# A gated encoder layer on one core: gate and up projections with the activation stationary instead of the weights

## The chip, the cores and the metric

The kernel runs on one core of a Trainium2 chip. The metric is the device time of one execution in microseconds. The time before is the median of three runs.

## The reference

One layer over 256 tokens of width 2048: a gated feed-forward network (FFN), two token mixers side by side with a gated merge, and a second FFN, each with norms around it. The change touches the two FFNs only.

```
def swiglu(h, w_gate, w_up, w_down):
    return (jax.nn.silu(h @ w_gate) * (h @ w_up)) @ w_down
...
f = swiglu(rmsnorm(x, ffn1_pre_g[l]), ffn1_w_gate[l], ffn1_w_up[l], ffn1_w_down[l])
x = x + 0.5 * rmsnorm(f, ffn1_post_g[l])
...
f = swiglu(rmsnorm(x, ffn2_pre_g[l]), ffn2_w_gate[l], ffn2_w_up[l], ffn2_w_down[l])
x = x + 0.5 * rmsnorm(f, ffn2_post_g[l])
```

w_gate and w_up are 2048 x 5632, w_down is 5632 x 2048, all float32.

## The kernel before

Every float32 operand is split into a high part (fp32r) and a low part, the rest. A product is three matmuls: high by high, low by high, high by low, summed in PSUM. The weights stream from memory once, in 728 **units** of 512 KB, in the order in which blocks use them (`add_block`, `add_block_T`). SyncE issues the loads (L147). ScalarE makes the high part of a unit (`whi`, L159) and VectorE the low part (`wlo`, L161). There are four buffers for the loaded unit (`raw`) and ten for the split ones, so five units are in store.

The 256 tokens are two halves `h` of 128. `xT` holds the transposed, split activations, 16 tiles of 128 rows by 256 tokens, in high and low. The norm's factor per token, `r_pre`, is not in `xT`; it is applied to the products.

There are two ways to run a block.

- `run_block` (L195): the activation is **stationary** (128 x 128) and 512 weight columns **move**. A unit is 256 rows by 512 columns. Per unit there are two halves, two row tiles and three matmuls (`mm3`, L169 to L171): 12 matmuls of 512 columns. A block over 2048 rows has 8 units, so 96 matmuls. The result has tokens on partitions and FFN columns along the free axis. All of the mixers, the down projections and the first 512 FFN columns (c == 0) run so.
- `run_block_T` (L225): the weights are **stationary**. A unit is 512 rows by 256 columns. The moving operand is `xT`: 512 columns (high and low of 256 tokens) against `whi`, then 256 columns (the high part) against `wlo`. A block makes 256 FFN columns for all tokens in 32 such pairs (L238 and L239; the last of each PSUM tile the other way round, L241 and L242). The result has FFN columns on partitions, which is the form in which the down projection wants its stationary operand, so nothing is transposed. The columns c = 1 to 10 of each FFN (512 wide, so two blocks `q` each for gate and for up) run so.

For c == 0, `up_after` multiplies (VectorE, L400) and `split_T` transposes the product on TensorE (L310), four tiles for each half, copies and splits it (L312, L313). For the other columns `sum_T` adds the two halves of a PSUM tile, a broadcast `r_bc` of the norm's factor is multiplied in (L415, L421), and silu, product and split follow. `r_bc` is made once for each FFN by `make_r_bc`, with two transposes (L372).

The FFN runs in two halves of its columns: gate and up of c = 0 to 5, their down projection, gate and up of c = 6 to 10, their down projection. The order on each engine is a schedule that is worked out when the kernel is built; the engines then run their queues in order.

Of the kernel before, what the change touches and what calls it, by code (L numbers as in the profile page):

```python
# [17 lines left out]
P = 128  # L18
# [24 lines left out]
def encoder_layer(  # L43
# [30 lines left out]
    def acc_tile():  # L74
        return accp.tile([P, NC], F32, tag="acc", name=nm("acc"))
# [26 lines left out]
    ident_r = const.tile([P, P], F32R, name="ident_r")  # L102
    sink = const.tile([P, NQ], F32, name="sink")
    nsink = const.tile([P, NQ], F32, name="nsink")
    r_bc = const.tile([P, SEQ], F32, name="r_bc")
    nlam = const.tile([P, 1], F32, name="nlam")
    mhalf = const.tile([P, 1], F32, name="mhalf")

# [12 lines left out]
    def add_block(w, r0, nu, c0):  # L121
        start = len(units)
        for u in range(nu):
            units.append(w[r0 + 256 * u:r0 + 256 * u + 256, c0:c0 + NC])
        return start

    def add_block_T(w, c0):
        start = len(units)
        for u in range(4):
            units.append(w[NC * u:NC * (u + 1), c0:c0 + 256])  # L130
        return start

    loaded, emitted = {}, {}
# [30 lines left out]
    def weights(k):  # L164
        emit_upto(k + LA)
        return emitted[k]
# [12 lines left out]
    def pump():  # L179
        for d in list(deferred):  # L180
            d[0] -= 1
            if d[0] <= 0:
                deferred.remove(d)
                d[1]()
        if ticker[0] is not None:
            try:
                next(ticker[0])
            except StopIteration:
                ticker[0] = None
# [31 lines left out]

    def quad(t, u):
        return t[:, :, 2 * (u % 2):2 * (u % 2) + 2, :]

    def run_block_T(start, after):  # L225
        """acc[m] = [W_m^T x_hi | W_m^T_hi x_lo] for two column tiles m of 128, tokens along the free axis."""
        acc = [acc_tile(), acc_tile()]
        for i in range(4):
            whi, wlo = weights(start + i)
            whi, wlo = (w.rearrange("p a b -> p (a b)").rearrange("p (j c) -> p j c", c=256) for w in (whi, wlo))  # L230
            for j in range(4):
                k = 4 * i + j
                xt = xT[k // 2][:, :, k % 2, :]
                for m in range(2):
                    a = whi[:, j, m * P:(m + 1) * P]
                    b = wlo[:, j, m * P:(m + 1) * P]
                    if k < 15:
                        nc.tensor.matmul(acc[m], a, xt, start=k == 0, stop=False)  # L238
                        nc.tensor.matmul(acc[m][:, 0:SEQ], b, xt[:, 0, :], start=False, stop=False)  # L239
                    else:  # L240
                        nc.tensor.matmul(acc[m][:, 0:SEQ], b, xt[:, 0, :], start=False, stop=False)  # L241
                        nc.tensor.matmul(acc[m], a, xt, start=False, stop=True)  # L242
            pump()
        after(acc)

    def rsqrt_of(ss, mul, add, tag):
        w = ss.shape[-1]
# [111 lines left out]
                nc.vector.tensor_tensor(fv, src, gb, ALU.mult)  # L359
            post_norm(f, pw, h, final)  # L360

    def sum_T(t, acc):
        for m in range(2):
            nc.scalar.copy(t[:, m], acc[m][:, SEQ:NC])  # L364
            nc.vector.tensor_tensor(t[:, m], acc[m][:, 0:SEQ], t[:, m], ALU.add)  # L365

    def make_r_bc():
        tp = tp_tile()
        for h in range(2):
            b = t2()[:, 0:P]  # L370
            nc.vector.tensor_copy(b, r_pre[h].to_broadcast([P, P]))
            nc.tensor.transpose(tp[:, h, :], b, ident)  # L372
        nc.vector.tensor_copy(r_bc.rearrange("p (h t) -> p h t", t=P), tp[:, 0:2, :])

    def ffn(post_g, pre, plan, lag, final, tail):
        hT = {}

        def hT_of(gu, h):
            if gu < 2:
                return quad(hT[0, h], gu)  # L380
            return hT[gu][:, :, :, h * P:(h + 1) * P]

        f = [[g4([2 * NC], F32) for _ in range(2)] for _ in range(2)]
        ss = [small(4, f"fss{h}") for h in range(2)]

        def lhs_h(off):
            return lambda u, h: hT_of(off + u, h)

        for half, (c_lo, c_hi) in enumerate(((0, 6), (6, 11))):
            for c in range(c_lo, c_hi):  # L390
                if c == 0:
                    s = [None, None]

                    def gate_after(h, acc):
                        s[h] = t2()
                        nc.scalar.activation(s[h], acc, AF.Silu, scale=r_pre[h])

                    def up_after(h, acc):
                        hh = t2()
                        nc.vector.scalar_tensor_tensor(hh, acc, r_pre[h], s[h], ALU.mult, ALU.mult)  # L400

                        def tr(h=h, hh=hh):
                            hT[0, h] = split_T(hh, 4, [2, 4, P])
                        later(tr, 1)
                    run_block(plan["gate"][c], KU, lhs_x, gate_after, lag, pre)
                    run_block(plan["up"][c], KU, lhs_x, up_after)
                    make_r_bc()
                    continue
                for q in (2 * c, 2 * c + 1):
                    st = [None]  # L410

                    def gate_T(acc):
                        t = st[0] = t2().rearrange("p (m t) -> p m t", t=SEQ)
                        sum_T(t, acc)
                        nc.vector.tensor_tensor(t, t, r_bc.unsqueeze(1).to_broadcast([P, 2, SEQ]), ALU.mult)  # L415
                        nc.scalar.activation(t, t, AF.Silu)

                    def up_T(acc):
                        t = t2().rearrange("p (m t) -> p m t", t=SEQ)
                        sum_T(t, acc)  # L420
                        nc.vector.tensor_tensor(t, t, r_bc.unsqueeze(1).to_broadcast([P, 2, SEQ]), ALU.mult)  # L421
                        nc.vector.tensor_tensor(t, t, st[0], ALU.mult)
                        o = hT[q] = g4([2, 2, SEQ])
                        nc.scalar.copy(o[:, 0], t)
                        nc.vector.tensor_tensor(o[:, 1], t, f32(o[:, 0]), ALU.subtract)
                    run_block_T(plan["gT", q], gate_T)
                    run_block_T(plan["uT", q], up_T)
            nu = 2 * (c_hi - c_lo)
            for n in range(4):
                gb = load_bc(post_g[0, n * NC:(n + 1) * NC]) if half == 1 else None  # L430
                last = half == 1 and n == 3

                def down_after(h, acc, n=n, gb=gb, last=last, half=half):
                    if half == 0:
                        nc.scalar.copy(f[h][n // 2][:, (n % 2) * NC:(n % 2) * NC + NC], acc)
                        return
                    finish_f(acc, f, gb, ss[h], h, n, True, 4.0 / D, 4.0 * EPS, final)
                run_block(plan["down"][half][n], nu, lhs_h(2 * c_lo), down_after, (LAG_END if final else LAG) if last else 0,
                          tail=tail if last else None)

    def plan_ffn(w_gate, w_up, w_down):
        pl = {"gate": {}, "up": {}, "down": [[], []]}
        for half, (c_lo, c_hi) in enumerate(((0, 6), (6, 11))):
            for c in range(c_lo, c_hi):
                if c == 0:
                    pl["gate"][c] = add_block(w_gate[0], 0, KU, 0)
                    pl["up"][c] = add_block(w_up[0], 0, KU, 0)
                    continue
                for q in (2 * c, 2 * c + 1):
                    pl["gT", q] = add_block_T(w_gate[0], q * 256)  # L450
                    pl["uT", q] = add_block_T(w_up[0], q * 256)
            for n in range(4):
                pl["down"][half].append(add_block(w_down[0], c_lo * NC, 2 * (c_hi - c_lo), n * NC))
        return pl
# [343 lines left out]


def _constants():  # L800
    """Rotary tables [cos, cos, -sin, sin] and window masks: functions of the shapes alone."""
    inv = np.float32(10000.0) ** (-np.arange(0, HD, 2, dtype=np.float32) / np.float32(HD))
    ang = np.arange(SEQ, dtype=np.float32)[:, None] * inv[None, :].astype(np.float32)
    c, s = np.cos(ang).astype(np.float32), np.sin(ang).astype(np.float32)
    rope = np.concatenate([c, c, -s, s], axis=1).reshape(2, P, 256).transpose(1, 0, 2)
    i = np.arange(P)
    keep = np.stack([i[None, :] <= i[:, None], i[None, :] >= i[:, None]], axis=1)
    mask = np.where(keep, np.float32(0), np.float32(NEG)).astype(np.float32)
    return np.ascontiguousarray(rope), np.ascontiguousarray(mask)
# [19 lines left out]
```

## Time and profile before

| | |
|---|---|
| runs | 2098.62, 2098.82, 2098.98 us, median 2098.82 us |
| profiled execution, span from first to last instruction | 2097.0 us |
| TensorE matmul busy | 2080.2 us, 99% |
| TensorE weight load busy | 1757.2 us, 84% |
| VectorE busy | 1253.5 us, 60% |
| ScalarE busy | 990.1 us, 47% |
| memory read | 187 GB/s over the span |

The profile gives the profiled execution's time as its span alone; it is 1.8 us under the median of the runs. Busy time of TensorE counts overlapped matmuls once, but the durations of single matmuls overlap their neighbours. What a matmul takes on the path is therefore read from start to start.

### The profile page before, as it was taken

What the parts mean: (1) busy time and instruction counts of PE and PEld (TensorE: products, weight loads), DVE (VectorE), ACT (ScalarE), POOL (GpSimd) and SP (SyncE); (2) the same over time, 40 slices, a digit from 0 to 9 for tenths busy, and PEclk for the clock granted to TensorE, in tenths of its full rate; (3) what the DMA queues carried; (4) which work ended last, traced back from release to release, by engine and by line L of the source; (5) the groups of instructions that cost most, each with busy time, mean ns of one, the idle gap of its engine ahead of it and who ended that gap; (6) DMA issues with size and microseconds to landing.
All of it is one profiled execution on the core that took longest, in us unless ns stands there. A gap on an engine that the chain in (4) does not pass through costs nothing.

```text
span 2097.0 us, 27165 instructions
## 1 busy us (share of the span) xinstructions
PE 2080.2 (99%) x10497; PEld 1757.2 (84%) x10497; DVE 1253.5 (60%) x1576; ACT 990.1 (47%) x1365; POOL 24.5 (1%) x41
## 2 busy tenths in 40 slices
PE   9999999999999999999999999999999999999998
PEld 6888888888888878888888888788888888888886
DVE  5665654456565576767755555666666445666655
ACT  6544444444444455554644444554444444444442
POOL 1000000000000000000000000000000000000000
PEclk9999999999999999999999999999999999999999
DMA  7665666666566656555466666566665666665663
GB/s 255 191 190 184 188 191 191 193 188 186 186 187 197 201 168 186 169 168 172 151 195 198 198 201 201 181 191 186 186 189 183 196 195 188 184 190 183 189 202 129
DMA packets 285680, 393.57 MB, mean 188 GB/s; under 512 B 12446, under 2 KB 177104, under 8 KB 285552
## 3 DMA queue, kind: packets, MB, share of 16 engines
q1 hardware_dynamic: 285136, 391.17, 60.6%
q8 instruction: 82, 1.34, 0.3%
q0 software_dynamic: 384, 0.68, 0.1%
q14 instruction: 46, 0.38, 0.0%
q10 hardware_dynamic: 32, 0.01, 0.0%
HBM read 389.71 MB, written 2.10 MB: 187 GB/s over the span
## 4 chain that ended last, share of the span: by engine, by line
PE 63%; issue 34%; DMA 1%; DVE 1%; ACT 1%; POOL 0%; SPq 0%; DVEq 0%; POOLq 0%; ACTq 0%
PE acc L238 13%; PE acc L170 13%; PE acc L171 13%; PE acc L169 13%; PE acc L239 7%; PE acc L242 1%; PE tp L310 0%; PE acc L241 0%; PE at L169 0%; DMA raw<-in_ffn_w_down 0%; PE tp L274 0%; PE at L171 0%; PE at L170 0%; DVE x_sb L323 0%; ACT whi L159 0%
## 5 line engine op out<-in xcount | busy, mean ns | idle before, releaser
L161 DVE TENSOR_TENSOR wlo<-raw,whi 128x1024 fp32r<-128x1024 f32 (+1 forms) x715 | 873.8, 1223 | 717.2 <-ACT whi L159 708.4
L159 ACT CAST whi<-raw 128x1024 fp32r<-128x1024 f32 (+1 forms) x715 | 751.1, 1051 | 860.1 <-PE acc L170 458.3
L238 PE MATMUL acc<-xT,whi 128*128 128x512 f32 x2400 | 851.3, 399 | 0.0
L239 PE MATMUL acc<-xT,wlo 128*128 128x256 f32 x2400 | 674.6, 281 | 0.0
L238 PEld LDWEIGHTS acc<-xT,whi 128*128 128x128 f32 x2400 | 451.0, 188 | 107.6
L239 PEld LDWEIGHTS acc<-xT,wlo 128*128 128x128 f32 x2400 | 453.7, 189 | 3.2
L170 PE MATMUL acc<-whi,g 128*128 128x512 f32 x928 | 361.2, 389 | 0.0
L169 PE MATMUL acc<-whi,g 128*128 128x512 f32 x928 | 361.1, 389 | 0.0
L171 PE MATMUL acc<-wlo,g 128*128 128x512 f32 x928 | 360.8, 389 | 0.0
L170 PE MATMUL acc<-whi,xT 128*128 128x512 f32 x648 | 255.7, 396 | 1.0 <-DVE xT L282 1.0
L169 PE MATMUL acc<-whi,xT 128*128 128x512 f32 x648 | 255.3, 395 | 0.3 <-ACT whi L159 0.3
L171 PE MATMUL acc<-wlo,xT 128*128 128x512 f32 x648 | 253.6, 394 | 0.0
L170 PEld LDWEIGHTS acc<-whi,g 128*128 128x128 f32 x928 | 174.2, 188 | 36.4
L171 PEld LDWEIGHTS acc<-wlo,g 128*128 128x128 f32 x928 | 174.2, 188 | 36.1
L169 PEld LDWEIGHTS acc<-whi,g 128*128 128x128 f32 x928 | 174.2, 188 | 35.9
L170 PEld LDWEIGHTS acc<-whi,xT 128*128 128x128 f32 x648 | 122.5, 189 | 25.3 <-DVE xT L282 1.7
L169 PEld LDWEIGHTS acc<-whi,xT 128*128 128x128 f32 x648 | 122.2, 189 | 25.1 <-ACT whi L159 0.8
L171 PEld LDWEIGHTS acc<-wlo,xT 128*128 128x128 f32 x648 | 122.4, 189 | 23.5
L364 ACT COPY t<-acc 128x256 f32<-128x256 f32 x160 | 60.0, 375 | 120.6 <-PE acc L242 120.6
L365 DVE TENSOR_TENSOR t<-acc,t 128x256 f32<-128x256 f32 x160 | 67.4, 421 | 52.4 <-ACT t L364 52.4
L242 PE MATMUL acc<-xT,whi 128*128 128x512 f32 x160 | 59.8, 396 | 0.0
L241 PE MATMUL acc<-xT,wlo 128*128 128x256 f32 x160 | 45.3, 283 | 0.0
(159 smaller groups left out, 942.7 us busy)
## 6 DMA issues: line engine op xcount, KB each, us to landing
raw<-in_ffn_w_up SPq DMA_DIRECT2D x176, 512.0 KB, 3.6
raw<-in_ffn_w_down SPq DMA_DIRECT2D x176, 512.0 KB, 3.7
raw<-in_ffn_w_gate SPq DMA_DIRECT2D x175, 512.0 KB, 3.6
raw<-in_w_in SPq DMA_DIRECT2D x136, 512.0 KB, 3.8
raw<-in_w_out SPq DMA_DIRECT2D x32, 512.0 KB, 3.7
raw<-in_w_proj_b SPq DMA_DIRECT2D x16, 512.0 KB, 4.5
raw<-in_w_proj_a SPq DMA_DIRECT2D x16, 512.0 KB, 4.2
bc<-in_ffn_post_g SPq DMA_DIRECT2D x8, 256.0 KB, 4.9
```

Of the source, the lines that this page charges most:

```text
L159: nc.scalar.copy(hi[:, j], raw[:, j])
L161: nc.vector.tensor_tensor(lo[:, j], raw[:, j], f32(hi[:, j]), ALU.subtract)
L169: nc.tensor.matmul(o, lhi, rhi, start=first, stop=False)
L170: nc.tensor.matmul(o, llo, rhi, start=False, stop=False)
L171: nc.tensor.matmul(o, lhi, rlo, start=False, stop=last)
L238: nc.tensor.matmul(acc[m], a, xt, start=k == 0, stop=False)
L239: nc.tensor.matmul(acc[m][:, 0:SEQ], b, xt[:, 0, :], start=False, stop=False)
L241: nc.tensor.matmul(acc[m][:, 0:SEQ], b, xt[:, 0, :], start=False, stop=False)
L242: nc.tensor.matmul(acc[m], a, xt, start=False, stop=True)
L364: nc.scalar.copy(t[:, m], acc[m][:, SEQ:NC])
L365: nc.vector.tensor_tensor(t[:, m], acc[m][:, 0:SEQ], t[:, m], ALU.add)
```

## The change

Gate and up of all eleven column groups run as c == 0 did: by `run_block`, with `silu` straight from PSUM (`gate_after`), the product from PSUM (`up_after`) and `split_T`, whose transposes come one step later (`later(tr, 1)`). `run_block_T`, `sum_T`, `make_r_bc`, `add_block_T` and `r_bc` go. Units of gate and up are all 256 rows by 512 columns now. Their number and size stay.

```diff
-                if c == 0:
-                    s = [None, None]
...
-                    run_block(plan["gate"][c], KU, lhs_x, gate_after, lag, pre)
-                    run_block(plan["up"][c], KU, lhs_x, up_after)
-                    make_r_bc()
-                    continue
-                for q in (2 * c, 2 * c + 1):
...
-                    def up_T(acc):
-                        t = t2().rearrange("p (m t) -> p m t", t=SEQ)
-                        sum_T(t, acc)
-                        nc.vector.tensor_tensor(t, t, r_bc.unsqueeze(1).to_broadcast([P, 2, SEQ]), ALU.mult)
-                        nc.vector.tensor_tensor(t, t, st[0], ALU.mult)
-                        o = hT[q] = g4([2, 2, SEQ])
-                        nc.scalar.copy(o[:, 0], t)
-                        nc.vector.tensor_tensor(o[:, 1], t, f32(o[:, 0]), ALU.subtract)
-                    run_block_T(plan["gT", q], gate_T)
-                    run_block_T(plan["uT", q], up_T)
+                s = [None, None]
+
+                def gate_after(h, acc, s=s):
+                    s[h] = t2()
+                    nc.scalar.activation(s[h], acc, AF.Silu, scale=r_pre[h])
+
+                def up_after(h, acc, s=s, c=c):
+                    hh = t2()
+                    nc.vector.scalar_tensor_tensor(hh, acc, r_pre[h], s[h], ALU.mult, ALU.mult)
+
+                    def tr():
+                        hT[c, h] = split_T(hh, 4, [2, 4, P])
+                    later(tr, 1)
+                run_block(plan["gate"][c], KU, lhs_x, gate_after, lag if c == 0 else 0, pre if c == 0 else None)
+                run_block(plan["up"][c], KU, lhs_x, up_after)
...
-                for q in (2 * c, 2 * c + 1):
-                    pl["gT", q] = add_block_T(w_gate[0], q * 256)
-                    pl["uT", q] = add_block_T(w_up[0], q * 256)
+                pl["gate"][c] = add_block(w_gate[0], 0, KU, c * NC)
+                pl["up"][c] = add_block(w_up[0], 0, KU, c * NC)
```

The instructions on TensorE at the border between an up block and the following gate block, in the first FFN (inside c = 1 before, from c = 1 to c = 2 after). The names are PSUM tiles (`acc`), split weights (`whi`, `wlo`) and transposed activations (`xT`). Before:

```order
L241 MATMUL acc_750<-xT_382,wlo_777 128x256
L242 MATMUL acc_750<-xT_382,whi_776 128x512
L241 MATMUL acc_751<-xT_382,wlo_777 128x256
L242 MATMUL acc_751<-xT_382,whi_776 128x512
L238 MATMUL acc_850<-xT_141,whi_798 128x512
L239 MATMUL acc_850<-xT_141,wlo_799 128x256
L238 MATMUL acc_851<-xT_141,whi_798 128x512
L239 MATMUL acc_851<-xT_141,wlo_799 128x256
```

After, at such a border:

```order
L162 MATMUL acc_795<-whi_888,xT_381 128x512
L163 MATMUL acc_795<-whi_888,xT_381 128x512
L164 MATMUL acc_795<-wlo_889,xT_381 128x512
L162 MATMUL acc_960<-whi_906,xT_140 128x512
L163 MATMUL acc_960<-whi_906,xT_140 128x512
L164 MATMUL acc_960<-wlo_907,xT_140 128x512
```

Pairs of 512 and 256 columns have become triples of 512.

TensorE again, in the second unit of that gate block, where the transposes of the finished up block now stand. Before, at that place in the block:

```order
L238 MATMUL acc_851<-xT_141,whi_798 128x512
L239 MATMUL acc_851<-xT_141,wlo_799 128x256
L238 MATMUL acc_850<-xT_166,whi_798 128x512
L239 MATMUL acc_850<-xT_166,wlo_799 128x256
L238 MATMUL acc_851<-xT_166,whi_798 128x512
L239 MATMUL acc_851<-xT_166,wlo_799 128x256
```

After:

```order
L164 MATMUL acc_960<-wlo_925,xT_165 128x512
L162 MATMUL acc_961<-whi_924,xT_165 128x512
L163 MATMUL acc_961<-whi_924,xT_165 128x512
L282 MATMUL tp_944<-ident,t_175_934 128x128 x4
L282 MATMUL tp_952<-ident,t_176_942 128x128 x4
L164 MATMUL acc_961<-wlo_925,xT_165 128x512
```

Eight transposes are new here. 20 matmuls stand between the last one of the up block and them (21 after c == 0), for every c of both FFNs.

VectorE over the end of an up block in the first FFN, where `t` is the gated product, `g` the split result for the down projection and `tp` the transposed tile. Before (second block `q` of a pair):

```order
L365 TENSOR_TENSOR t_184_1037<-acc_947,t_184_1037 128x256
L161 TENSOR_TENSOR wlo_1096<-raw_1093,whi_1095 128x1024
L365 TENSOR_TENSOR t_184_1037<-acc_948,t_184_1037 128x256
L421 TENSOR_TENSOR t_184_1037<-t_184_1037,r_bc 128x512
L422 TENSOR_TENSOR t_184_1037<-t_184_1037,t_169_940 128x512
L161 TENSOR_TENSOR wlo_1118<-raw_1115,whi_1117 128x1024
L425 TENSOR_TENSOR g_185_1044<-t_184_1037,g_185_1044 128x512
```

After:

```order
L154 TENSOR_TENSOR wlo_1299<-raw_1296,whi_1298 128x1024
L353 SCALAR_TENSOR_TENSOR t_235_1250<-acc_1110,pnr_392,t_207_1100 128x512
L353 SCALAR_TENSOR_TENSOR t_236_1258<-acc_1111,pnr_407,t_208_1108 128x512
L154 TENSOR_TENSOR wlo_1317<-raw_1314,whi_1316 128x1024
L154 TENSOR_TENSOR wlo_1335<-raw_1332,whi_1334 128x1024
L285 TENSOR_TENSOR g_238_1265<-tp_1260,g_238_1265 128x512
L285 TENSOR_TENSOR g_240_1273<-tp_1268,g_240_1273 128x512
```

The two products come at once, two weight splits follow, and then the two splits of the transposed tiles.

## Rows read from the trace of the kernel before

**Rows 1.** The page: engine busy time with instructions, and TensorE's granted clock in 40 slices.

```profile
PE 2080.2 (99%) x10497; PEld 1757.2 (84%) x10497; DVE 1253.5 (60%) x1576; ACT 990.1 (47%) x1365; POOL 24.5 (1%) x41
PEclk9999999999999999999999999999999999999999
```

**Rows 2.** Waits of TensorE: who for whom, us in total, times, longest.

```profile
PE acc L170 <- DVE xT L282: 2.7, 5, 0.8
PE tp L274 <- DMA x_sb<-in_x: 1.9, 1, 1.9
PE acc L116 <- DVE warm L113: 1.2, 1, 1.2
PE acc L169 <- ACT xT L280: 0.6, 1, 0.6
PE acc L169 <- ACT whi L159: 0.3, 1, 0.3
```

**Rows 3.** TensorE's groups by form: count, busy us, mean ns of one.

```profile
L238 PE MATMUL acc<-xT,whi 128*128 128x512 f32 x2400 | 851.3, 399 | 0.0
L239 PE MATMUL acc<-xT,wlo 128*128 128x256 f32 x2400 | 674.6, 281 | 0.0
...
L170 PE MATMUL acc<-whi,xT 128*128 128x512 f32 x648 | 255.7, 396 | 1.0 <-DVE xT L282 1.0
...
L310 PE MATMUL tp<-ident,t 128*128 128x128 f32 x96 | 14.0, 272 | 0.0
```

**Rows 4.** TensorE's timeline: first matmuls of two neighbouring weight-stationary blocks (start, us).

```profile
83.87 0.39 PE L238 MATMUL acc<-xT,whi 128*128 128x512 f32 x1
...
95.17 0.39 PE L238 MATMUL acc<-xT,whi 128*128 128x512 f32 x1
```

**Rows 5.** Busy time by stretch: weight-stationary block, mixer's gate block, down projection.

```profile
83.87:95.17 11.30, 11.30 (x66) 9.82 (x64) 7.56 (x9) 5.37 (x8) 0.00 (x0) 1.00 0.60 186
...
1081.54:1103.30 21.76, 21.76 (x97) 18.02 (x96) 11.19 (x11) 9.48 (x11) 0.00 (x0) 1.00 0.67 205
...
350.00:372.00 22.00, 22.00 (x99) 18.22 (x98) 9.80 (x8) 9.74 (x11) 0.00 (x0) 1.00 0.61 192
```

The columns of rows 5 are the stretch, its length, then busy us and instructions of TensorE, its weight loads, VectorE, ScalarE and GpSimd, then the granted clock, the DMA share and GB/s.

**Rows 6.** TensorE's timeline: borders of activation-stationary blocks in the mixer.

```profile
1081.54 0.39 PE L169 MATMUL acc<-whi,xT 128*128 128x512 f32 x1
...
1103.30 0.39 PE L169 MATMUL acc<-whi,g 128*128 128x512 f32 x1
...
1125.06 0.39 PE L169 MATMUL acc<-whi,xT 128*128 128x512 f32 x1
...
1147.72 0.39 PE L169 MATMUL acc<-whi,xT 128*128 128x512 f32 x1
```

**Rows 7.** TensorE's timeline: eight transposes inside such a block.

```profile
1130.73 0.39 PE L170 MATMUL acc<-whi,xT 128*128 128x512 f32 x1
1130.96 1.03 PE L310 MATMUL tp<-ident,t 128*128 128x128 f32 x8
1131.75 0.48 PE L171 MATMUL acc<-wlo,xT 128*128 128x512 f32 x1
1132.07 0.40 PE L169 MATMUL acc<-whi,xT 128*128 128x512 f32 x1
```

**Rows 8.** TensorE's timeline: the transposes of `make_r_bc` in the second FFN.

```profile
1403.62 0.38 PE L372 MATMUL tp<-ident,t 128*128 128x128 f32 x2
```

**Rows 9.** Timelines of TensorE and VectorE: the c == 0 up block's end, second FFN.

```profile
1394.13 0.39 PE L171 MATMUL acc<-wlo,xT 128*128 128x512 f32 x1
...
1393.84 1.54 DVE L400 SCALAR_TENSOR_TENSOR t<-acc,pnr,t 128x512 f32<-128x512 f32 x2
...
1398.11 1.04 PE L310 MATMUL tp<-ident,t 128*128 128x128 f32 x8
```

**Rows 10.** Waits of ScalarE before it splits a unit: us in total, times, longest.

```profile
ACT whi L159 <- PE acc L170: 458.3, 301, 2.6
ACT whi L159 <- PE acc L238: 187.6, 125, 2.3
...
ACT whi L159 <- DMA raw<-in_ffn_w_gate: 4.2, 5, 1.6
```

More of the change, by code (lines that the diff above doesn't have):

```diff
@@ L104, in encoder_layer @@
     nsink = const.tile([P, NQ], F32, name="nsink")
-    r_bc = const.tile([P, SEQ], F32, name="r_bc")
     nlam = const.tile([P, 1], F32, name="nlam")
@@ L124, in add_block @@
             units.append(w[r0 + 256 * u:r0 + 256 * u + 256, c0:c0 + NC])
[L125 to L130, printed above, removed]
         return start
@@ L223, in quad @@
         return t[:, :, 2 * (u % 2):2 * (u % 2) + 2, :]
[L225 to L244, printed above, removed]
     def rsqrt_of(ss, mul, add, tag):
@@ L360, in finish_f @@
             post_norm(f, pw, h, final)
[L362 to L373, printed above, removed]
     def ffn(post_g, pre, plan, lag, final, tail):
         hT = {}
[L378 to L381, printed above, removed]
         f = [[g4([2 * NC], F32) for _ in range(2)] for _ in range(2)]
@@ L386, in lhs_h @@
         def lhs_h(off):
-            return lambda u, h: hT_of(off + u, h)
+            return lambda u, h: quad(hT[(off + u) // 2, h], off + u)
         for half, (c_lo, c_hi) in enumerate(((0, 6), (6, 11))):
             for c in range(c_lo, c_hi):
-                if c == 0:
-                    s = [None, None]
[L394 to L404, printed above, removed]
-                    run_block(plan["gate"][c], KU, lhs_x, gate_after, lag, pre)
-                    run_block(plan["up"][c], KU, lhs_x, up_after)
-                    make_r_bc()
-                    continue
-                for q in (2 * c, 2 * c + 1):
-                    st = [None]
-                    def gate_T(acc):
-                        t = st[0] = t2().rearrange("p (m t) -> p m t", t=SEQ)
-                        sum_T(t, acc)
-                        nc.vector.tensor_tensor(t, t, r_bc.unsqueeze(1).to_broadcast([P, 2, SEQ]), ALU.mult)
-                        nc.scalar.activation(t, t, AF.Silu)
-                    def up_T(acc):
-                        t = t2().rearrange("p (m t) -> p m t", t=SEQ)
-                        sum_T(t, acc)
-                        nc.vector.tensor_tensor(t, t, r_bc.unsqueeze(1).to_broadcast([P, 2, SEQ]), ALU.mult)
-                        nc.vector.tensor_tensor(t, t, st[0], ALU.mult)
-                        o = hT[q] = g4([2, 2, SEQ])
-                        nc.scalar.copy(o[:, 0], t)
-                        nc.vector.tensor_tensor(o[:, 1], t, f32(o[:, 0]), ALU.subtract)
-                    run_block_T(plan["gT", q], gate_T)
-                    run_block_T(plan["uT", q], up_T)
@@ L444, in plan_ffn @@
             for c in range(c_lo, c_hi):
[L445 to L448, printed above, removed]
-                for q in (2 * c, 2 * c + 1):
-                    pl["gT", q] = add_block_T(w_gate[0], q * 256)
-                    pl["uT", q] = add_block_T(w_up[0], q * 256)
+                pl["gate"][c] = add_block(w_gate[0], 0, KU, c * NC)
+                pl["up"][c] = add_block(w_up[0], 0, KU, c * NC)
             for n in range(4):
```

## Prediction

> **What bounds the kernel now.** I first read the busy shares. TensorE is busy for 2080.2 of 2097.0 us and its granted clock stands in the top tenth in all 40 slices [rows 1]. VectorE and ScalarE have 40% and 53% of the span free. Busy shares prove little, so the list of waits comes next: TensorE waits for others for 6.7 us in all, in nine waits [rows 2]. So the kernel is TensorE's instruction stream, back to back, and a change is worth what it changes in the length of that stream, unless it brings in waits. The third view is the groups by form [rows 3], from which the reader should take the counts only. A 512-column matmul shows 389 to 399 ns and a transpose 272 ns, but these durations overlap their neighbours; the sum of all would be far longer than the span. The price on the path is the distance from start to start, best taken over a whole block.
>
> Such distances stand in the timeline. A weight-stationary block runs from 83.87 to 95.17 us, 11.30 us [rows 4]. It has 32 pairs, so a pair of 512 and 256 columns takes 353 ns. The activation-stationary form does not have to be guessed, since the mixer's gate blocks run exactly what the change puts in: `xT` stationary, 512 columns of `whi` or `wlo` moving, 8 units, 96 matmuls. One runs from 1081.54 to 1103.30, 21.76 us [rows 6], thus 226.7 ns per matmul. The granted clock is 1.00 in both stretches, the upper of its two levels, 2.4 GHz [rows 5].
>
> **The change, part by part.**
>
> *Gate and up.* A column group c of 512 columns now takes four weight-stationary blocks, 4 x 11.30 = 45.20 us. After, it takes two blocks, 2 x 21.76 = 43.52 us. The columns that move are the same, 49,152 for each block of 512 FFN columns (64 x 768 and 96 x 512). What falls is the number of matmuls, from 64 pairs, 128, to 96. At 2.4 GHz the columns alone are 20.48 us, and what lies above them is 2.12 us before and 1.28 us after, 16.6 and 13.3 ns for each matmul. So the price hangs on the matmuls as well as on the columns. Gain 1.68 us for each c, ten c in each of two FFNs: 33.6 us.
>
> *The transposes.* Each of the 20 column groups adds eight transposes on TensorE, 160 in all. Their price on the path is in the same mixer: the gate block from 1125.06 to 1147.72, 22.66 us, holds eight transposes of the same line as the new ones [rows 6], against 21.76 without. That is 0.90 us for eight, 0.11 each. The detail agrees: the eight begin at 1130.96, the next matmul starts at 1131.75, and the one after it is some 0.1 us late [rows 7]. 20 x 0.90 = 18.0 us. As a lower bound I take 0.79 us for eight, the stretch that they fill themselves.
>
> The Trainium skill, in "TensorE: Matmul & The Clock Gate", section "Part 4: PE-mode transpose", gives about 275 ns for a transpose inside a kernel. The mean of 272 ns in [rows 3] agrees with it as a duration; by it, added up, 160 transposes would be 44.0 us and the change a loss of 9.9 us. By the distances of [rows 6] they are 18.0 us, and I go by these.
>
> *What goes.* `make_r_bc` has two transposes in each FFN [rows 8]; at 0.11 us that is 0.45 us for both. On VectorE go four half-tile additions, the multiplications by `r_bc`, and more, on ScalarE the copies; in their place come two products from PSUM and the split of two transposed tiles. Both engines get less to do, and neither is waited for [rows 2], so I cost this at nothing.
>
> *The new wait.* The first transpose waits for VectorE's product, and everything behind it on TensorE waits with it, since the queue runs in order. The order puts 20 matmuls between the up block and the transposes, so they come 21 x 0.227 = 4.8 us after the last up matmul starts. How long the product takes is seen at c == 0: the last up matmul starts at 1394.13, both products are done at 1393.84 + 1.54 = 1395.38, and the transposes start at 1398.11 without a wait [rows 9]. So 1.25 us are needed and 4.8 are there, 3.5 us to spare. In VectorE's queue one weight split may lie ahead of the product (some 1.2 us), which is still covered. The weight splits behind the products feed units that TensorE reaches over 5 us later. Cost 0; if the cover went, each 0.1 us of wait would cost 2 us over the 20 groups.
>
> *Weight supply.* A unit is used up in 11.30 / 4 = 2.83 us before and 21.76 / 8 = 2.72 us after. That faster pace is already held in the mixer and in the down projections, where TensorE has no gap at 205 and 192 GB/s and DMA shares of 0.67 and 0.61 [rows 5]. ScalarE begins to split a unit when TensorE frees its buffers (645.9 us of waits in 426 cases, against 4.2 us for a load of gate weights) [rows 10]: loads run ahead, not behind. The rows of a load grow from 256 to 512 columns, the form that the mixer's weights have. Cost 0.
>
> *Sum.* -33.6 + 18.0 - 0.45 = -16.05 us. The profiled execution's span becomes 2097.0 - 16.05 = 2080.95; with the 1.8 us by which the median of the runs is longer, **2082.8 us**, 0.76% less than 2098.82.
>
> **The rivals.**
>
> 1. *Columns alone.* If TensorE's time went by columns, and the 0.84 us between 22.60 and 21.76 belonged to the mixer's surroundings, the blocks would stay as long and only the transposes be added: 2098.8 + 18.0 - 0.45 = 2116.4 us, slower by 0.8%. It decides once the gain for a c is under 0.88 us. Against it: same clock, same operands, same column count in [rows 4, 6], and the down projection's matmuls run at the mixer's pace too [rows 5].
> The Trainium skill, same page, section "Back-to-back issue gap", has a rule close to this one: a warm matmul takes N / 2.4 + 2.5 ns from start to start. By it 64 pairs are 20.80 us and 96 matmuls 20.72, the gain 0.16 us for a c, and with the transposes of [rows 6] the change loses 14.4 us. The trace contradicts it: 353 ns for a pair where the rule gives 325, and 226.7 where it gives 215.8.
> 2. *Transposes at their full duration*, if they do not overlap their neighbours here: 160 x 0.272 = 43.5 us, 2098.8 - 33.6 - 0.45 + 43.5 = 2108.3 us. It decides when eight cost over 1.70 us. [rows 6, 7] speak against it, from the same line of code among the same matmuls.
> 3. *TensorE waits at the transposes.* With the longest wait for VectorE in [rows 2], 0.8 us, at each of the 20 places: +16 us, 2098.8 us, no change. The 3.5 us of slack speak against it.
> 4. *Supply holds the old pace*, 2.83 us per unit: blocks stay at 45.20 us for a c, transposes vanish in the waits, 2098.4 us, no change. [rows 5, 10] speak against it.
>
> **How the numbers follow.** The forecast has 0.86, rival 1 0.02, rival 2 0.03, rivals 3 and 4 0.09 together; half of that I take for a part of the wait only, which leaves a gain above 4 us. A change of 0.2%, 4.2 us, is about what can be told from none. Faster: 0.86 + 0.04 = 0.90; same 0.05; slower 0.05. The range: below, eight transposes at 0.79 us give 2.2 us more, 2080.6, and I go a microsecond further for small gains; above, a wait of 0.2 us at each group adds 4 us, 2086.8. So 2079.5 to 2087.
>
> **What the new profile would show.** TensorE with 9373 matmuls (of the 10497 [rows 1], 20 x 56 and the four of `make_r_bc` go), 160 more transposes in the group of `split_T`, no idle before them; one block every 21.76 us in gate and up, 22.66 us where transposes lie; DVE and ACT busy less. The forecast is wrong if such a block is longer: then either the matmuls inside are over 227 ns apart (rival 1), or the gap around the eight transposes is over 1 us (2, 3), or a `whi` or `wlo` ends a wait of TensorE at a unit's first matmul (4).

## The result and the profile after

The kernel after takes 2082.88 us, the median of four runs (2082.13 to 2083.59), against 2098.72 us before in the same comparison (2097.86 to 2098.98). The ratio is 0.9925 with a 95% interval of 0.9911 to 0.9939: faster, by 15.8 us. The profiled execution has a span of 2081.2 us; the forecast was 2080.95 for it and 2082.8 for the median.

The page of the kernel after, busy times and granted clock, to hold against [rows 1]:

```profile
PE 2064.4 (99%) x9373; PEld 1708.8 (82%) x9373; DVE 1141.7 (55%) x1330; ACT 948.8 (46%) x1205; POOL 24.5 (1%) x41
PEclk9999999999999999999999999999999999999999
```

TensorE is as full as before, with the granted clock again in the top tenth, and has 1124 matmuls fewer: its stream became shorter. VectorE and ScalarE have less to do. The list of waits of TensorE after (who for whom, us in total, times, longest), against [rows 2]:

```profile
PE acc L163 <- DVE xT L254: 2.2, 4, 0.8
PE tp L246 <- DMA x_sb<-in_x: 1.4, 1, 1.4
PE acc L115 <- DVE warm L112: 1.2, 1, 1.2
PE tp L246 <- DVE x_sb L295: 0.6, 1, 0.6
PE acc L162 <- ACT xT L252: 0.6, 1, 0.6
PE acc L162 <- ACT whi L152: 0.2, 1, 0.2
```

The six rows add up to 6.2 us, where it was 6.7, and none of it is at the new transposes (L282). The price of a block is in TensorE's timeline after, at the first matmuls of three neighbouring blocks (start, us): up of c = 1, gate of c = 2, up of c = 2.

```profile
82.18 0.39 PE L162 MATMUL acc<-whi,xT 128*128 128x512 f32 x1
...
103.94 0.39 PE L162 MATMUL acc<-whi,xT 128*128 128x512 f32 x1
...
126.59 0.39 PE L162 MATMUL acc<-whi,xT 128*128 128x512 f32 x1
```

Up takes 21.76 us and gate, which holds the eight transposes, 22.65 us: 44.41 us for a column group, where four blocks of [rows 4] took 45.20. Twenty times 0.79 is 15.8 us. The inside of that gate block in the same timeline, and VectorE's timeline ahead of it:

```profile
103.72 0.39 PE L164 MATMUL acc<-wlo,xT 128*128 128x512 f32 x1
...
108.48 1.03 PE L282 MATMUL tp<-ident,t 128*128 128x128 f32 x8
109.27 0.48 PE L164 MATMUL acc<-wlo,xT 128*128 128x512 f32 x1
```

```profile
103.42 1.47 DVE L353 SCALAR_TENSOR_TENSOR t<-acc,pnr,t 128x512 f32<-128x512 f32 x2
```

The products are done at 103.42 + 1.47 = 104.89 and the transposes begin at 108.48, 3.6 us later. In the other groups of both FFNs it is 3.5 or 3.6 us.

### The profile page after: what moved, and what is told of

It is laid out like the page before. It is cut to its first block, busy times and chain, and to the rows that moved or that the text cites. A ratio compares the mean times of both kernels' runs of the same rounds, so it can differ in the third digit from the quotient of the medians.

```text
span 2081.2 us, 24436 instructions
## 1 busy us (share of the span) xinstructions
PE 2064.4 (99%) x9373; PEld 1708.8 (82%) x9373; DVE 1141.7 (55%) x1330; ACT 948.8 (46%) x1205; POOL 24.5 (1%) x41
## 4 chain that ended last, share of the span: by engine, by line
PE 63%; issue 34%; DMA 1%; DVE 1%; ACT 1%; POOL 0%; POOLq 0%; DVEq 0%; ACTq 0%
PE acc L163 20%; PE acc L164 20%; PE acc L162 20%; PE tp L282 1%; DMA raw<-in_w_in 0%; PE at L162 0%; PE at L163 0%; PE at L164 0%; DVE x_sb L295 0%; PE tp L246 0%; DMA sink<-in_sink_logit 0%; ACT whi L152 0%; DMA raw<-in_ffn_w_down 0%; DMA raw<-in_ffn_w_up 0%; DVE g L154 0%
## 5 line engine op out<-in xcount | busy, mean ns | idle before, releaser
L163 PE MATMUL acc<-whi,xT 128*128 128x512 f32 x1928 | 754.1, 392 | 0.7 <-DVE xT L254 0.6
L162 PE MATMUL acc<-whi,xT 128*128 128x512 f32 x1928 | 754.1, 392 | 0.2 <-ACT whi L152 0.2
L164 PE MATMUL acc<-wlo,xT 128*128 128x512 f32 x1928 | 753.5, 392 | 0.0
L163 PEld LDWEIGHTS acc<-whi,xT 128*128 128x128 f32 x1928 | 362.7, 188 | 75.1 <-DVE xT L254 1.7
L162 PEld LDWEIGHTS acc<-whi,xT 128*128 128x128 f32 x1928 | 362.7, 188 | 74.1 <-ACT xT L252 0.8
L164 PEld LDWEIGHTS acc<-wlo,xT 128*128 128x128 f32 x1928 | 362.8, 188 | 73.1 <-DVE wlo L154 0.3
L285 DVE TENSOR_TENSOR g<-tp,g 128x512 fp32r<-128x512 f32 (+1 forms) x68 | 42.2, 653 | 19.3 <-ACT g L284 19.3
L284 ACT CAST g<-tp 128x512 fp32r<-128x512 f32 (+1 forms) x68 | 35.4, 563 | 36.8 <-PE tp L282 36.4
L349 ACT ACTIVATE t<-acc,pnr 128x512 f32<-128x512 f32 x44 | 30.2, 686 | 10.5 <-PE acc L164 10.5
L282 PE MATMUL tp<-ident,t 128*128 128x128 f32 x256 | 34.6, 272 | 0.0
L282 PEld LDWEIGHTS tp<-ident,t 128*128 128x128 f32 x256 | 30.2, 140 | 5.2
L353 DVE SCALAR_TENSOR_TENSOR t<-acc,pnr,t 128x512 f32<-128x512 f32 x44 | 32.4, 748 | 0.0
```

The costliest lines, as they stand in the source:

```text
L162: nc.tensor.matmul(o, lhi, rhi, start=first, stop=False)
L163: nc.tensor.matmul(o, llo, rhi, start=False, stop=False)
L164: nc.tensor.matmul(o, lhi, rlo, start=False, stop=last)
L282: nc.tensor.transpose(tp[:, j, :], src[:, j * P:(j + 1) * P], ident)
L284: nc.scalar.copy(t[:, 0, :, :], tp[:, 0:n, :])
L285: nc.vector.tensor_tensor(t[:, 1, :, :], tp[:, 0:n, :], f32(t[:, 0, :, :]), ALU.subtract)
```

## The experiments

Nine kernels ran. Each is compared with runs of the kernel before on the same chip. The second and the third ran only once and have no ratio; there the length of a block in the trace carries the reading. A matmul of 512 moving columns is called wide here, one of 256 narrow.

**The transposes left out.** In the kernel after, the gated product is split without being transposed, so the down projection reads an untransposed operand; this kernel leaves the transposition out and does not compute the layer.

```diff
-                        hT[c, h] = split_T(hh, 4, [2, 4, P])
+                        t = hT[c, h] = g4([2, 4, P])
+                        s4 = hh.rearrange("p (j q) -> p j q", q=P)
+                        nc.scalar.copy(t[:, 0, :, :], s4)
+                        nc.vector.tensor_tensor(t[:, 1, :, :], s4, f32(t[:, 0, :, :]), ALU.subtract)
```

> The kernel after, but the gated product goes to the split without being transposed (so the down projection reads an operand that is not transposed: that part of the computation is changed). All 22 column groups lose their eight transposes. Theory of the prediction (0.90 us on TensorE's path for eight): 22 x 0.90 = 19.8 us less than 2082.9, so 2063.1 us. Rival, transposes cost their full duration of 272 ns: 176 x 0.272 = 47.9 us less, 2035. Rival, they are hidden: 2082.9.

Measured 2063.89 us (2062.48 to 2065.03, four runs), ratio to before 0.9828 (0.9812 to 0.9844). That is 19.0 us under the kernel after; 19.8 were expected, and the difference is within the spread of the runs. The transposes are neither hidden nor do they cost what their records last: the 272 ns of a record overlap their neighbours, the path pays 19.0 us / 176 = 0.11 us.

**The narrow matmuls made wide.** In the kernel before, the matmul against `wlo` gets 512 moving columns too (the same edit in both branches of the loop).

```diff
-nc.tensor.matmul(acc[m][:, 0:SEQ], b, xt[:, 0, :], start=False, stop=False)
+nc.tensor.matmul(acc[m], b, xt, start=False, stop=False)
```

> The kernel before, with 512 moving columns in the matmul against wlo too (it adds the product of the two low parts), so all 5120 matmuls of the weight-stationary blocks are 512 wide. If every matmul costs its columns at 2.4 GHz and a fixed 13.3 ns, as in the activation-stationary blocks, two take 453.4 ns in place of 353.1: +256.8 us, 2355.6. If a 512-column matmul of the weight-stationary form takes the 236 ns that it has in the pair: 472.6 ns, +305.9 us, 2404.7.

Measured 2355.03 us. That is the first theory (2355.6) and not the second (2404.7). TensorE's timeline of this kernel, two borders of blocks:

```profile
89.13 0.39 PE L238 MATMUL acc<-xT,whi 128*128 128x512 f32 x1
...
103.64 0.39 PE L238 MATMUL acc<-xT,whi 128*128 128x512 f32 x1
```

14.51 us for 64 matmuls are 226.7 ns each. Weights stationary or activation stationary, a 512-column matmul among its like costs the same. Here, too, every second matmul adds into the PSUM tile that the one before it wrote, and pays nothing for it.

**The wide matmuls cut in two.** In the kernel after, for c = 1 to 10, gate and up run through this in place of `mm3`:

```diff
+    def mm6(o, lhi, llo, rhi, rlo, first, last):
+        for l, r, st, sp in ((lhi, rhi, first, False), (llo, rhi, False, False), (lhi, rlo, False, last)):
+            for q in (slice(0, NC),) if st or sp else (slice(0, SEQ), slice(SEQ, NC)):
+                nc.tensor.matmul(o[:, q], l, r[:, q], start=st, stop=sp)
```

> The kernel after, with the 512-column matmuls of gate and up for c = 1 to 10 cut into two of 256 (all but the first and last of each PSUM tile): 188 in place of 96 in each of 40 blocks, same columns. Fixed cost of 13.3 ns for each matmul: a 256 takes 120.0 ns, a block 22.99 us in place of 21.76, +49.2 us, 2132. If a 256 takes the 116.8 ns that it has in the pair of before: 22.40 us, +25.6 us, 2108.5. If columns alone count: 2082.9.

Measured 2131.37 us, against 2132, 2108.5 and 2082.9: the fixed price for each matmul. Two borders in its timeline:

```profile
83.33 0.63 PE L169 MATMUL acc<-whi,xT 128*128 128x512 f32 x3
...
106.32 0.51 PE L169 MATMUL acc<-whi,xT 128*128 128x512 f32 x2
```

The block is 22.99 us long, as worked out: 4 matmuls of 226.7 and 184 of 120.0 ns. Between 256 and 512 columns lie 106.7 ns, exactly 256 columns at 2.4 GHz, and 13.3 ns remain at either width. Each matmul has a weight load of its own in all these kernels (13053 of both in this one), so the 13.3 ns are the price of a matmul together with its load; the runs do not divide it.

**One piece in place of two.** In the kernel before, `xT` is laid out so that the high and the low part of a row tile lie side by side.

```diff
-                xT[u] = xTp.tile([P, 2, 2, SEQ], F32R, tag="xT", name=nm("xT"))
+                xT[u] = xTp.tile([P, 2, 2, SEQ], F32R, tag="xT", name=nm("xT")).rearrange("p k a s -> p a k s")
```

> The kernel before, with xT laid out so that the 512 moving columns of L238 (high and low part of one row tile) lie in one piece instead of two pieces of 256. Theory of the prediction (a price for each matmul, whatever its operand's layout): no change, 2098.8. Rival: the two pieces cost the 512-column matmul the 9.6 ns by which 236.3 lies over 226.7: 2560 x 9.6 = 24.6 us less, 2074.2.

Measured 2099.22 us (ten runs), ratio 1.0001 (0.9992 to 1.001). The layout of the moving operand is not it.

This leaves a remainder. A pair of 512 and 256 columns should cost 226.7 + 120.0 = 346.7 ns and takes 353.1 [rows 4]. The runs so far say that neither the form nor the layout makes these 6.4 ns. Three kernels change only the order of the matmuls in the kernel before.

**Groups of two.**

```diff
-                for m in range(2):
...
+                for f_ in (hi, lo) if k < 15 else (lo, hi):
+                    f_(0)
+                    f_(1)
```

> The kernel before, with its matmuls in another order: for each row tile the two of 512 columns, then the two of 256. Same matmuls, same columns. A pair costs 353.1 ns; columns and 13.3 ns for each matmul make 346.7, so 6.4 ns a pair are left. Theory A, each change of width between neighbours costs (two changes a pair before, one here): half of 6.4 ns x 2560, 8.2 us less, 2090.6. Theory B, it is the 256 that adds into the PSUM tile that the 512 just before it wrote: all of it goes, 16.4 us less, 2082.4. Theory C, it belongs to the weight-stationary form whatever the order: 2098.8.

Measured 2087.92 us, ratio 0.9945 (0.9927 to 0.9963). Two borders of blocks in its timeline, 11.17 us apart:

```profile
81.70 1.09 PE L235 MATMUL acc<-xT,whi 128*128 128x512 f32 x4
...
92.87 1.09 PE L235 MATMUL acc<-xT,whi 128*128 128x512 f32 x4
```

**Groups of eight.**

```diff
-            for j in range(4):
...
+            for f_ in (hi, lo) if i < 3 else (lo, hi):
+                for j in range(4):
+                    for m in range(2):
+                        f_(j, m)
```

> The kernel before, with the matmuls of a unit in groups of one width: eight of 512 columns, then eight of 256 (the other way round in a block's last unit). Theory A, each change of width costs: seven eighths of 16.4 us less, 14.3 us, 2084.5. Theory B, adding into the PSUM tile just written: 16.4 us less, 2082.4, as in the run with groups of two. Theory C, the form: 2098.8.

Measured 2087.15 us, ratio 0.9943 (0.9927 to 0.9959). Theory C is out: the form has no such price, the order has. But neither A nor B fits: groups of two bring more than A allows (10.7 us against 8.2), groups of eight less than both (11.4 against 14.3 and 16.4). The timeline of the kernel with groups of eight shows where the rest is:

```profile
84.04 1.11 PE L238 MATMUL acc<-xT,wlo 128*128 128x256 f32 x8
84.99 2.00 PE L233 MATMUL acc<-xT,whi 128*128 128x512 f32 x8
86.83 1.12 PE L238 MATMUL acc<-xT,wlo 128*128 128x256 f32 x8
87.79 2.00 PE L233 MATMUL acc<-xT,whi 128*128 128x512 f32 x8
...
95.19 1.12 PE L238 MATMUL acc<-xT,wlo 128*128 128x256 f32 x8
```

The first narrow ones of two neighbouring blocks are 95.19 - 84.04 = 11.15 us apart. Eight wide matmuls after narrow ones take 84.99 to 86.83, 1.84 us, where 8 x 226.7 ns are 1.81; the eight narrow ones 0.95 to 0.96 where 8 x 120.0 are 0.96. From start to start, the first five wide ones take 233, 236, 228, 233 and 231 ns (in the group from 87.79 on), then it is 227; the first narrow one after wide ones takes 113. So in groups of eight a return from narrow to wide costs about 20 ns net, spread over five matmuls. This made theory D, tried next.

**Widths turned round from unit to unit.** As the last, with one line changed.

```diff
-            for f_ in (hi, lo) if i < 3 else (lo, hi):
+            for f_ in (hi, lo) if i % 2 == 0 else (lo, hi):
```

> The kernel before, with the widths turned round from unit to unit (eight of 512, sixteen of 256, sixteen of 512, and so on), so that a block comes back from 256 to 512 columns twice in place of three times. New theory D, from the trace of the run with groups of eight: what is lost is paid by the first five 512-column matmuls after a return from 256 (27 ns together, of which 6 come back at the first 256), about 20 ns for each return; block 32 x 346.7 ns + 2 x 20 ns = 11.13 us in place of 11.15, 1.6 us less than that run, 2085.5. Theory C (the form): a block as in the run with groups of eight, 2087.2. In either case not under the kernel after, 2082.9.

Measured 2085.34 us (2083.93 to 2086.52), ratio 0.9935 (0.9918 to 0.9951), 1.8 us under groups of eight. The intervals of the two ratios overlap, so the ratios alone would not carry it; the block in the trace is 95.35 - 84.22 = 11.13 us, as worked out, where groups of eight have 11.15, groups of two 11.17 and the kernel before 11.30.

```profile
84.22 2.08 PE L238 MATMUL acc<-xT,wlo 128*128 128x256 f32 x16
...
95.35 2.08 PE L238 MATMUL acc<-xT,wlo 128*128 128x256 f32 x16
```

The 20 ns are not a price for every return. Over the 11.09 us that 32 x 346.7 ns make, groups of two lose about 0.08 us in 16 returns, 5 ns each, and the kernel before 0.21 us in 32, 6.4 ns each: a shorter group of wide matmuls pays less per return and has more returns. Why a return to the wide ones costs this stays open.

**The product made late.** In the kernel after, three more passes of VectorE over each gated product.

```diff
+                    for _ in range(3):
+                        nc.vector.tensor_scalar_mul(hh, hh, 1.0)
```

> The kernel after, with three more passes of VectorE over each gated product (times 1.0) before it is transposed: some 4 us later for the two halves, more than the 3.5 us to spare; the order puts the transposes 37 places behind the up block in place of 21. Theory of the prediction (TensorE's stream alone sets the time, VectorE has room): 2082.9, no change. Rival, the wait at the transposes or VectorE's load counts: 20 groups and 4 us each would be up to 80 us more; 0.2 us each would be 2086.9.

Measured 2083.21 us (2082.22 to 2083.50), ratio 0.9923 (0.9908 to 0.9939): no change to the kernel after. VectorE's load is no part of the time. Of the wait the run says little. The schedule put the transposes 16 places further back, and the delay was smaller than expected. TensorE's and VectorE's timelines at the end of the up block of c = 1:

```profile
102.91 0.39 PE L164 MATMUL acc<-wlo,xT 128*128 128x512 f32 x1
...
111.30 1.03 PE L282 MATMUL tp<-ident,t 128*128 128x128 f32 x8
...
105.48 1.76 DVE L355 TENSOR_SCALAR t<-t 128x512 f32<-128x512 f32 x5
```

The last matmul of the up block starts at 102.91 and the products are done at 107.24, 4.33 us later; in the kernel after it is 104.89 - 103.72 = 1.17. So they came 3.2 us later, not 4, and would have been 0.4 us ahead of the transposes at their old place as well. A kernel in which the product comes too late was not tried, and what such a wait would cost is not shown.

**A smaller stock of weights.** In the kernel after, four units in store in place of five, and three loads in place of four.

```diff
-    rawp = ctx.enter_context(tc.tile_pool(name="rawp", bufs=4))
-    wp = ctx.enter_context(tc.tile_pool(name="wp", bufs=10))
+    rawp = ctx.enter_context(tc.tile_pool(name="rawp", bufs=3))
+    wp = ctx.enter_context(tc.tile_pool(name="wp", bufs=8))
```

> The kernel after with three buffers in place of four for loaded units and eight in place of ten for split ones (four units in store). If loads and splits run ahead of TensorE, as the prediction has it: no change in the FFN blocks, 2082.9, at most a few us at the stage borders. If the weight supply is close to being the bound at 2.72 us per unit (rival 4): blocks of gate and up get longer than 21.76 us, and 0.1 us more for each unit would be 73 us over the 728 units.

Measured 2097.61 us (2095.89 to 2098.75, ten runs), ratio to before 0.9992 (0.9983 to 1.0002): 14.7 us slower than the kernel after, all of the gain. "At most a few us at the borders" was wrong in size, though not in place. The same up block as above, in this kernel's timeline, and its waits of TensorE:

```profile
83.85 0.39 PE L162 MATMUL acc<-whi,xT 128*128 128x512 f32 x1
...
105.61 0.39 PE L162 MATMUL acc<-whi,xT 128*128 128x512 f32 x1
```

```profile
PE tp L246 <- DVE x_sb L295: 8.8, 2, 5.5
PE tp L246 <- DMA x_sb<-in_x: 2.8, 1, 2.8
```

The block is still 21.76 us, and the block borders run 1.7 us behind the kernel after from the start of the FFN on to its down projection without a further loss. Most of the time goes at the two borders where one norm ends and the next begins. Matmul by matmul against the kernel after, the 14.1 us between the two profiled spans (2095.3 and 2081.2) are 1.7 us by the first blocks of the first FFN, 6.0 at the border to the mixers, 5.7 at the border to the second FFN and 0.7 at the end. At the two borders TensorE waits 8.8 us for the updated `x_sb`, 0.6 in the kernel after. Two more losses stand behind these waits. In TensorE's timeline at the first border and, in the last row, at the second (between the square brackets, the idle time before an instruction):

```profile
751.19 1.08 PE L246 MATMUL tp<-ident,x_sb 128*128 128x128 f32 x4 [5.45 <-DVE x_sb L295]
752.31 0.79 PE L162 MATMUL acc<-g,xT 128*128 128x512 f32 x1
752.95 0.80 PE L163 MATMUL acc<-g,xT 128*128 128x512 f32 x1
753.55 0.63 PE L164 MATMUL acc<-g,xT 128*128 128x512 f32 x1
753.98 0.63 PE L162 MATMUL acc<-g,xT 128*128 128x512 f32 x1
754.40 0.50 PE L163 MATMUL acc<-g,xT 128*128 128x512 f32 x1
754.74 0.39 PE L164 MATMUL acc<-g,xT 128*128 128x512 f32 x1
...
772.18 0.50 PE L162 MATMUL acc<-whi,xT 128*128 128x512 f32 x1 [0.52 <-ACT whi L152]
...
773.44 0.51 PE L164 MATMUL acc<-wlo,xT 128*128 128x512 f32 x1 [0.30 <-DVE wlo L154]
...
1348.46 1.05 PE L246 MATMUL tp<-ident,x_sb 128*128 128x128 f32 x4 [3.38 <-DVE x_sb L295]
```

And its busy time at both borders, in the columns of [rows 5]:

```profile
747.80:754.60 6.80, 3.38 (x9) 2.25 (x10) 6.39 (x13) 2.19 (x5) 3.59 (x4) 0.50 0.51 158
...
1348.55:1351.90 3.35, 3.35 (x9) 2.13 (x10) 2.98 (x10) 1.15 (x4) 0.55 (x1) 0.50 0.65 212
```

TensorE stands idle for 5.45 us up to 751.19 and for 3.38 us up to 1348.46. In the two stretches shown, one that begins within the first idle time and one right after the second, the granted clock is 0.50, the lower of its two levels. Five wide matmuls take 2.43 us there (752.31 to 754.74), where 5 x 226.7 ns are 1.13. In the kernel after, the clock is 1.00 at both places. Some 20 us behind each of the waits TensorE waits 0.8 us more for a `whi` and a `wlo`; the kernel after has one such wait of 0.2 us in all. So rival 4 is ruled out where the change is, and the stock of weights is needed elsewhere. Which of the two stocks does it, loaded or split, and why the smaller one makes `x_sb` late, is not shown.

## Why the prediction was right

*TensorE's stream sets the time.* It held: no wait at the new transposes, a granted clock of 1.00 in the blocks, as before, and the time followed the stream in every run but the one with the smaller stock.

*Gate and up, -33.6 us.* 21.76 us for a block, as forecast from the mixer's block. Here the sum was right and one reading in it was too coarse. The prediction spread what lies above the columns over the matmuls, 16.6 ns each before and 13.3 after. The runs show 13.3 ns for each matmul in both forms, as long as its neighbours are of its width. Of the 0.84 us that a block of 512 FFN columns gains (22.60 to 21.76), 32 matmuls fewer are 32 x 13.3 ns = 0.43 us, and the other half, 64 x 6.4 ns = 0.41 us, comes from widths that no longer alternate. The sum did not suffer from this, since it goes by the lengths of whole blocks. Half of the blocks' gain could have been had by reordering, and 80 blocks of 11.13 us show most of it: 2085.34 us, 13.8 us less than before, where the whole change, which has to pay for transposes, brings 15.8.

*The transposes, +18.0 us.* 0.89 us for eight in the trace after (22.65 - 21.76), 0.90 forecast; 19.0 us for all 22 groups by leaving them out, 19.8 by the forecast's price.

*`make_r_bc`, -0.45 us.* Gone; 0.45 us is less than the spread of the runs, so it is not measured by itself. With it the terms as measured come to -33.6 + 17.8 - 0.45 = -16.25 us, 0.4 more than the 15.8 found, which is within that spread too.

*The new wait, 0.* 3.6 us to spare, 3.5 forecast, and no idle time before the transposes.

*Weight supply, 0.* Right in gate and up at 2.72 us per unit, and still right with four units in store.

*The rivals.* Columns alone: out by the cut matmuls, which move the same columns and take 48.5 us more. Transposes at full duration: out by leaving them out. The waits: not in the trace.

The Trainium skill's rule of 2.5 ns over the columns, which it gives for a matmul by itself ("TensorE: Matmul & The Clock Gate", section "Back-to-back issue gap"), would have made this change a loss by the prediction's estimate. This case's traces have 13.3 ns at 256 and at 512 columns, so the measurement decides against it here: by that constant 32 matmuls fewer are worth an estimated 0.08 us, by the traces 0.43.

## What to carry to other kernels

When TensorE is full and has no waits, count its matmuls, not only its columns, and take the price of each form from start to start over a whole block of the same trace; durations of records overlap and mislead, of transposes most of all. Two forms of one product that move the same columns can differ by nearly 4% of a block (22.60 and 21.76 us here). If narrow and wide matmuls must be mixed, put those of one width together before anything larger is rebuilt.

## What the runs showed that was not expected

- Alternating 512 and 256 columns costs 6.4 ns a pair over the sum of what each costs among its like (353.1 against 346.7 ns). Reordering alone, in groups of eight and turned round from unit to unit, gave ratios of 0.9943 and 0.9935 to the kernel before, where the whole change gives 0.9925.
- After eight or sixteen narrow matmuls the next five wide ones each take 1 to 9 ns more than 226.7.
- One unit less in store and one load less in flight cost 14.7 us, most of it at two borders of stages, while the blocks between them kept their length to 0.01 us. Where TensorE stood idle there for 5.45 and 3.38 us, the granted clock was 0.50 for 6.8 and 3.4 us.
